# Expert weights of two mixture-of-experts blocks in loads of two megabytes instead of one

## The chip, the cores and the metric

The kernel runs on one core of a Trainium2 chip, and the figure is the device time of one execution in microseconds, the median of several runs. All arithmetic of the experts is in 32-bit floats.

## The reference, cut to what matters

Two transformer blocks run one after the other on 256 tokens of width 1024. Each ends in a layer of experts, and every expert's weights are read once from HBM:

```python
# first block: 16 experts, each takes its 32 best tokens
xg = jax.vmap(lambda hb, ib: hb[ib])(h, idx)                     # (1, 16, 32, 1024)
hid = jax.nn.silu(jnp.einsum('becd,edf->becf', xg, w_gate)) * jnp.einsum('becd,edf->becf', xg, w_up)
y = jnp.einsum('becf,efd->becd', hid, w_down) * gate[..., None]  # w_gate, w_up: 1024x2048; w_down: 2048x1024
...
# second block: 32 experts of width 512, two for each token, at most 64 rows of an expert in the fast path
hid = jax.nn.silu(xb @ w1[e]) * (xb @ w3[e])                     # w1, w3: 1024x512; w2: 512x1024
return hid @ w2[e]
```

That is 24 MB of weights for each of the 16 experts of the first block (384 MB) and 6 MB for each of the 32 of the second (192 MB); "MB" is 1,048,576 bytes here and in the prediction, where a load is spoken of. All else (attention mixers, projections, norms) needs some 115 MB.

## The kernel before

The program is four functions in a row: `block1` (mixers of the first block), `experts1`, `block2` (mixers of the second), `experts2`.

**Loads.** All weights come through `K.load` (line 211): it takes the next of a list of pools, `self.rings`, each one buffer of 8 KB in every partition, and lets SyncE's queue issue one DMA of 128 partitions by 8 KB, 1 MB. SyncE issues in order. A load waits until the readers of the buffer's last tile are done; it also waits for the load eight before it to land, since eight semaphores go round. `program` (line 2009) opens four buffers for good. `extra_ring` adds more while memory is free, `turn` rotates the list. When `experts1` begins, the list holds 19 buffers: 10 of the 11 opened ahead of the output projection of `block1`, the four, the eleventh, and four opened at that block's end. For `experts2` it holds 18: seven opened inside `block2`, seven at its end, and the four. The scheduler lets loads go ahead of their use as soon as buffers allow, so each ring is filled while the output projection and the router ahead of its experts still run.

**First block's experts** (`experts1`, line 1248 on): groups `gq` of four experts. `rows` gathers the tokens of a group into `xg` (two copies, `bufs=2`) by one-hot matmuls `gx`. For each expert, `G` (gate) and `U` (up) take eight loads each; each load feeds four matmuls that fill four stripes of 32 partitions (each is shown as two instructions in the trace). `hs` = silu(G)·U, `hT` its transpose, and `Yp` takes eight loads of `w_down`. These come from HBM as two rows of 4 KB for each partition, since `w_down` lies there as in the reference; `w_gate` and `w_up` have rows of 8 KB. The last expert takes `w_down` by halves of the columns, in four rows of 2 KB. Then `cmb` matmuls add the result to `x1`.

**Second block's experts** (`experts2`, line 1760 on): eight turns `e0` of four experts, each in two steps `c` of two experts; a step takes four loads of `w1` into `G`, four of `w3` into `U`, four of `w2` into `Yp`, all in rows of 8 KB that `layout` has packed.

Of the kernel before, what the change touches and what calls it, by code (L numbers as in the profile page):

```python
# [9 lines left out]
F32 = mybir.dt.float32  # L10
# [90 lines left out]
def layout(I):  # L101
# [37 lines left out]
    w = I["w_in"][0]  # L139
# [13 lines left out]
    A["w_choose"] = wpack(np.concatenate([I["w_group_2"][0], I["w_expert_2"][0]], 1), (0,), 36)[0]  # L153
    for n in ("w_gate", "w_up", "w_down"):
        A[n] = I[n][0]
    w = I["w_in_2"][0]
# [10 lines left out]
    for n in ("w1", "w3"):  # L167
        A[n] = I["moe_" + n + "_2"][0].reshape(16, 2, 4, 2, 128, 512).transpose(0, 2, 4, 3, 1, 5).reshape(64, 128, 2048)
    A["w2"] = I["moe_w2_2"][0].reshape(16, 2, 2, 2, 128, 2, 512).transpose(0, 5, 2, 4, 3, 1, 6).reshape(64, 128, 2048)
    return {k: np.ascontiguousarray(v) for k, v in A.items()}  # L170
# [3 lines left out]
class K:  # L174
# [14 lines left out]
    def setup(self):  # L189
        nc = self.nc  # L190
        self.rings = [self.pool("ring") for _ in range(self.ring_n)]
        self.nload = 0
# [68 lines left out]
    def extra_ring(self, n, head=0):  # L261

        st, old = ExitStack(), self.rings
        k = len(old) - head
        self.rings, self.nload = old[:k] + [self.pool("ring2", st=st) for _ in range(n)] + old[k:], 0
        st.callback(lambda: setattr(self, "rings", old))
        return st

    def turn(self, n):

        self.rings, self.nload = self.rings[n:] + self.rings[:n], 0

# [210 lines left out]
def block1(S):  # L483
# [667 lines left out]
    main.close()  # L1151
    ring = S.extra_ring(11)

# [5 lines left out]
    st.close()  # L1159
    S.turn(S.ring_n)  # L1160
    S.turn(1)
    ring.callback(S.extra_ring(4).close)
    return x1, ring


def experts1(S, x1, ring):
# [81 lines left out]
    for gq in range(4):  # L1248
        xg = lb.tile([128, 8, 128], F32, name="xg", bufs=2)

# [12 lines left out]
        for ee in range(4):  # L1263
# [4 lines left out]
            for wn, p in (("w_gate", G), ("w_up", U)):  # L1268
                for k in range(8):
                    wt = S.load(I[wn][e, 128 * k:128 * k + 128, :], wn)  # L1270
                    for j in range(4):
                        mm(p[32 * j:32 * j + 32, :], xg[:, k, s_], wt[:, 512 * j:512 * j + 512], k == 0, k == 7)
            if ee == 0:
# [28 lines left out]
            if not last:  # L1302
                for i in range(8):
                    wt = S.load(I["w_down"][e, 256 * i:256 * i + 256, :].rearrange("(k p) d -> p k d", k=2), "w_down")
                    for kk in range(2):
                        j, b = (2 * i + kk) // 4, (2 * i + kk) % 4
                        for n in range(2):
                            lo = 64 * kk + 32 * n
                            mm(Yp[lo:lo + 32, :], hT[:, b, 32 * j:32 * j + 32], wt[:, 1024 * kk + 512 * n:1024 * kk + 512 * n + 512], i == 0, i == 7)
# [52 lines left out]
def block2(S, x):  # L1362
# [301 lines left out]
    ring.close()  # L1664
    ring = S.extra_ring(7)

# [27 lines left out]
    st.close()  # L1694
    S.turn(S.ring_n)
    more = S.extra_ring(7, S.ring_n)
    ring.callback(more.close)
# [19 lines left out]
def experts2(S, x, ring, out):  # L1717
# [127 lines left out]
    def gate_up(xg, e0, c):  # L1845
# [3 lines left out]
        for wn, p in (("w1", G), ("w3", U)):  # L1849
            for k in range(0, 8, 2):  # L1850
                wt = S.load(I[wn][2 * (e0 + 2 * c) + k // 2], wn)
                for kk in range(2):
                    for e in range(2):
# [14 lines left out]

    def down(Y, hT, e, n, qs=(0, 2)):

        for q in qs:
            wt = S.load(I["w2"][2 * e + 2 * n + q // 2], "w2")
            for b in range(2):
                for i in range(2):
                    lo = 1024 * b + 512 * i
                    pe(Y[64 * i:64 * i + 64, n, :], hT[:, q + b, 64 * i:64 * i + 64], wt[:, lo:lo + 512], q + b == 0, q + b == 3)

# [26 lines left out]
    for e0 in range(0, 32, 4):  # L1904
# [34 lines left out]
        Y = py.tile([128, 2, 512], F32, name="Yp")  # L1939
        down(Y, hT, 30, 0)  # L1940
        yb = [evac(Y, 0, gs[:, 1:2])]
        down(Y, hT, 30, 1, (0,))
        for k in range(4):
            add(k, [(ya, sel[:, 0]), (yb, sel[:, 1])])
        down(Y, hT, 30, 1, (2,))
        yb.append(evac(Y, 1, gs[:, 1:2]))
# [18 lines left out]
    with tc.If(nover > 0):  # L1965
# [7 lines left out]
        with tc.For_i(0, 16, 1) as i:  # L1973
            def weights(wn, ab, name):

                t = so.tile([128, 2, 2, 512], F32, name=name, tag=name)
                nc.sync.dma_start(t, I[wn].rearrange("(i c) p f -> i c p f", c=4)[bass.ds(i, 1), ab].rearrange("a p f -> p (a f)"))
                return t
# [64 lines left out]
```

## Time and profile before

| | |
|---|---|
| median of 3 runs | 2084.6 us (2080.07 to 2085.31) |
| profiled execution, its own time | 2084.64 us |
| its span (first to last instruction) | 2082.8 us |
| TensorE (PE) busy | 1704.7 us, 82% |
| HBM read | 720.96 MB (10^6 bytes), 347 GB/s over the span |
| chain that ended last | DMA 48%, PE 37%, VectorE 8%, ScalarE 3% |
| loads of the experts | w 192, w_gate 128, w_up 128, w_down 128, 1024 KB each |

The span falls into stretches: `block1` up to about 389 us, `experts1` to about 1308, `block2` to about 1616, `experts2` to the end. The median and the profiled execution agree to 0.04 us, so sums are made against 2084.64 us, which is the span and 1.84 us around it.

### The profile page before, as it was taken

The page shows a single profiled execution, that of the slowest core. Times are in us where ns is not written, and L with a number is a line of the kernel's source. Part 1 is how long each engine was busy: PE and PEld are TensorE (multiplying, and loading weights), DVE is VectorE, ACT ScalarE, POOL GpSimd, SP SyncE. Part 2 cuts the span into 40 slices and gives each one's busy share as a digit, 9 for nine tenths or more (in the row PEclk, how much of TensorE's full clock was granted, in tenths as well). Part 3 has the DMA queues.
Part 4 walks back from the last instruction along what each step waited for, and adds up shares of the span by engine and source line. Part 5 has one row for each costly group of instructions (what it writes and reads, how often), then busy time and mean ns, then how long its engine had stood idle before and what let it go on. Part 6 is the DMA issues. An engine that isn't in the chain of part 4 may idle for free.

```text
span 2082.8 us, 25800 instructions
## 1 busy us (share of the span) xinstructions
PE 1704.7 (82%) x10570; PEld 845.0 (41%) x10570; DVE 672.3 (32%) x1327; ACT 448.6 (22%) x797; POOL 211.9 (10%) x273
## 2 busy tenths in 40 slices
PE   5979999876776667666676776899998999999997
PEld 1657557411211112111121111788998444444443
DVE  4797674311111111001011110699655112222212
ACT  4632325200010001000010000476644111111111
POOL 2334432000000000000000000243101000000000
PEclk8989999887787787877877778899999999999998
DMA  7356649799999999999999999434557799999995
GB/s 308 114 192 263 219 169 393 320 424 423 425 425 425 425 423 425 424 424 425 425 425 425 424 424 418 174 134 144 218 200 310 323 426 427 426 426 427 426 427 224
DMA packets 120842, 723.75 MB, mean 347 GB/s; under 512 B 11456, under 2 KB 13248, under 8 KB 50448
## 3 DMA queue, kind: packets, MB, share of 16 engines
q1 hardware_dynamic: 119600, 717.97, 84.2%
q0 software_dynamic: 1120, 4.08, 0.6%
q8 instruction: 85, 1.39, 0.2%
q14 instruction: 37, 0.30, 0.0%
HBM read 720.96 MB, written 1.05 MB: 347 GB/s over the span
## 4 chain that ended last, share of the span: by engine, by line
DMA 48%; PE 37%; DVE 8%; ACT 3%; issue 2%; POOL 1%; SPq 0%; DVEq 0%; ACTq 0%; POOLq 0%
DMA w_up<-in_w_up_dram 14%; DMA w_gate<-in_w_gate_dram 13%; DMA w_down<-in_w_down_dram 13%; DMA w<-in_w_dram 8%; PE pj L253 7%; PE Yp L1809 4%; PE U L1809 3%; PE G L1809 3%; PE pw L253 2%; PE U L1179 2%; DVE tmp L781 1%; PE mp L514 1%; PE ya L253 1%; PE gx L1809 1%; PE yb L253 1%
## 5 line engine op out<-in xcount | busy, mean ns | idle before, releaser
L1179 PE MATMUL U<-w_up,xg 128*32 128x512 f32 x1024 | 199.8, 872 | 99.9 <-DMA w_up<-in_w_up_dram 99.9
L1179 PE MATMUL Yp<-w_down,hT 128*32 128x512 f32 x1024 | 175.2, 785 | 91.5 <-DMA w_down<-in_w_down_dram 81.3
L1179 PE MATMUL G<-w_gate,xg 128*32 128x512 f32 x1024 | 159.0, 664 | 55.1 <-DMA w_gate<-in_w_gate_dram 54.9
L1285 DVE TENSOR_TENSOR hs<-hs,U 128x512 f32<-128x512 f32 x16 | 11.0, 687 | 469.6 <-PE U L1179 469.6
L1179 PEld LDWEIGHTS U<-w_up,xg 128*32 128x32 f32 x1024 | 24.7, 127 | 274.2 <-DMA w_up<-in_w_up_dram 243.1
L253 PE MATMUL pj<-uh,whi 128*128 128x256 f32 x408 | 118.1, 290 | 3.2 <-ACT uh L1409 3.2
L1809 PE MATMUL U<-w,xg 128*64 128x512 f32 x512 | 115.3, 595 | 5.8 <-DMA w<-in_w_dram 5.8
L253 PE MATMUL pj<-uh,wlo 128*128 128x256 f32 x408 | 116.8, 286 | 1.1 <-DVE wlo L235 1.1
L253 PE MATMUL pj<-ul,whi 128*128 128x256 f32 x408 | 115.7, 284 | 0.0
L1809 PE MATMUL Yp<-w,hT 128*64 128x512 f32 x512 | 113.8, 596 | 2.2 <-DVE ysl L1882 1.6
L1179 PEld LDWEIGHTS Yp<-w_down,hT 128*32 128x32 f32 x1024 | 25.5, 124 | 215.5 <-DMA w_down<-in_w_down_dram 187.4
L1809 PE MATMUL G<-w,xg 128*64 128x512 f32 x512 | 112.6, 592 | 0.0
L1299 ACT COPY ys<-Yp 128x256 f32<-128x256 f32 x17 | 6.3, 372 | 486.7 <-DVE ys L1298 486.7
L234 ACT CAST whi<-win 128x1024 fp32r<-128x1024 f32 x72 | 75.0, 1045 | 95.4 <-PE pj L253 61.6
L1179 PE MATMUL cmb<-seln,ys 128*128 128x256 f32 x256 | 85.6, 470 | 11.6 <-DVE ys L1298 9.5
L1422 POOL DMA_DIRECT2D dist<-in_dist_dram x1 | 0.6, 608 | 908.8 <-PE tq L436 908.8
L1179 PEld LDWEIGHTS G<-w_gate,xg 128*32 128x32 f32 x1024 | 27.8, 114 | 152.7 <-DMA w_gate<-in_w_gate_dram 108.6
L1298 DVE COPY ys<-Yp 128x256 f32<-128x256 f32 x17 | 7.2, 424 | 246.3 <-PE Yp L1179 246.3
L1295 DVE SCALAR_TENSOR_TENSOR x<-cmb,modT,x 128x256 f32<-128x256 f32 x128 | 59.4, 484 | 68.1 <-PE cmb L1179 68.1
L1179 PEld LDWEIGHTS cmb<-seln,ys 128*128 128x128 f32 x256 | 50.2, 221 | 76.2 <-DVE ys L1298 29.7
L253 PEld LDWEIGHTS pj<-uh,whi 128*128 128x128 f32 x408 | 77.6, 191 | 5.2 <-ACT uh L1409 3.5
L253 PEld LDWEIGHTS pj<-uh,wlo 128*128 128x128 f32 x408 | 77.5, 190 | 2.5 <-DVE wlo L235 1.5
(564 smaller groups left out, 2942.3 us busy)
## 6 DMA issues: line engine op xcount, KB each, us to landing
w<-in_w_dram SPq DMA_DIRECT2D x192, 1024.0 KB, 19.5
w_gate<-in_w_gate_dram SPq DMA_DIRECT2D x128, 1024.0 KB, 19.6
w_up<-in_w_up_dram SPq DMA_DIRECT2D x128, 1024.0 KB, 19.6
w_down<-in_w_down_dram SPq DMA_DIRECT2D x128, 1024.0 KB, 19.6
wmod<-in_w_mod_dram SPq DMA_DIRECT2D x48, 1024.0 KB, 6.0
win<-in_w_in_dram SPq DMA_DIRECT2D x36, 1024.0 KB, 4.9
wout<-in_w_out_dram SPq DMA_DIRECT2D x8, 1024.0 KB, 6.4
wrnn<-in_w_rnn_out_dram SPq DMA_DIRECT2D x8, 640.0 KB, 7.2
```

Of the source, the lines that this page charges most:

```text
L234: self.nc.scalar.copy(hi, x)
L253: self.nc.tensor.matmul(out, a(k), b(k), start=(n == 0), stop=(n == 3 * K - 1))
L514: nc.tensor.matmul(out, l, r, start=a, stop=b)
L781: nc.vector.tensor_tensor(tv, X[:, 0:i, 0:i], bc(Lt[:, None, 0:i, i], [128, i, i]), op=ALU.mult)
L1179: nc.tensor.matmul(out, l, r, start=a, stop=b)
L1285: nc.vector.tensor_tensor(hs, hs, U, op=ALU.mult)
L1295: nc.vector.scalar_tensor_tensor(x1[:, k, :], pc, S.modT[:, 40 + k, 0:1], x1[:, k, :], op0=ALU.mult, op1=ALU.add)
L1298: nc.vector.tensor_copy(ys[:, 0:256], Y[:, 0:256])
L1299: nc.scalar.copy(ys[:, 256:512], Y[:, 256:512])
L1422: nc.gpsimd.dma_start(dist, I["dist"])
L1809: tc.keep_in_program_order(nc.tensor.matmul(o, l, r, start=a, stop=b))
```

## The change

- Weights of all experts are packed by `layout` so that 16 KB stand in a row for each partition; a load is 128 rows of 16 KB, 2 MB. `w_gate` and `w_up` take four loads for an expert instead of eight, `w_down` four whole rows instead of eight pairs of 4 KB rows. The last expert of the first block keeps eight loads of 1 MB for `w_down`, now one row of 8 KB each instead of four of 2 KB. In the second block `w1`, `w3` and `w2` take two loads for a step instead of four; the last step keeps four loads of 1 MB for `w2`.
- The list of buffers becomes a list of windows of 16 KB, each a pool used as a small ring (`windows`); `room` puts a load of 2 MB, or two of 1 MB, into a window. All other loads stay at 1 MB.
- The counts: 10 + 4 + 6 buffers of 8 KB for the first block's experts, that is 10 windows (20 MB instead of 19), and 6 + 8 + 4, 9 windows, for the second's (18 MB as before). `xg` of the first block has one copy instead of two.

```diff
+    for n in ("w_gate", "w_up"):
+        A[n] = I[n][0].reshape(16, 4, 2, 128, 2048).transpose(0, 1, 3, 2, 4).reshape(64, 128, 4096)
+    w = I["w_down"][0].reshape(16, 4, 4, 128, 1024).transpose(0, 1, 3, 2, 4).reshape(64, 128, 4096)
+    w[60:] = I["w_down"][0, 15].reshape(2, 8, 128, 2, 512).transpose(3, 0, 2, 1, 4).reshape(4, 128, 4096)
...
+    def windows(self, n, st):
+        out = []
+        for i in range(0, n, 2):
+            m = min(2, n - i)
+            out.append((self.pool("ring", st=st).ring(8192 * m), m))
+        return out
+
+    def room(self, need, name):
+        i, used = self.place
+        while used + need > self.rings[i][1]:
+            i, used = (i + 1) % len(self.rings), 0
+        self.place = (i, used + need)
+        return self.rings[i][0].tile([128, 2048 * need], F32, name=name)
+
     def load(self, src, name):
-        pool = self.rings[self.nload % len(self.rings)]
-        self.nload += 1
-        t = pool.tile([128, 2048], F32, name=name, tag="w")
+        t = self.room(2 if math.prod(src.shape[1:]) > 2048 else 1, name)
...
-    ring = S.extra_ring(11)
+    ring = S.extra_ring(10)
...
-    ring.callback(S.extra_ring(4).close)
+    ring.callback(S.extra_ring(6).close)
...
-        xg = lb.tile([128, 8, 128], F32, name="xg", bufs=2)
+        xg = lb.tile([128, 8, 128], F32, name="xg", bufs=1)
...
-                    wt = S.load(I[wn][e, 128 * k:128 * k + 128, :], wn)
+                    if k % 2 == 0:
+                        wt = S.load(I[wn][4 * e + k // 2], wn)
...
-                for i in range(8):
-                    wt = S.load(I["w_down"][e, 256 * i:256 * i + 256, :].rearrange("(k p) d -> p k d", k=2), "w_down")
+                for i in range(4):
+                    wt = S.load(I["w_down"][4 * e + i], "w_down")
...
-                    wt = S.load(I["w_down"][e, 512 * i:512 * i + 512, 512 * n:512 * n + 512].rearrange("(k p) d -> p k d", k=4), "w_down")
+                    wt = S.load(I["w_down"][4 * e + 2 * n + i // 2, :, 2048 * (i % 2):2048 * (i % 2) + 2048], "w_down")
...
-    ring = S.extra_ring(7)
+    ring = S.extra_ring(6)
...
-    more = S.extra_ring(7, S.ring_n)
+    more = S.extra_ring(8, S.ring_n // 2)
...
-            for k in range(0, 8, 2):
-                wt = S.load(I[wn][2 * (e0 + 2 * c) + k // 2], wn)
+            for k in range(0, 8, 4):
+                wt = S.load(I[wn][e0 + 2 * c + k // 4], wn)
...
+    def down(Y, hT, e, n, q=0, c=4):
+        wt = S.load(I["w2"][e + n, :, 1024 * q:1024 * (q + c)], "w2")
```

The order of SyncE's queue where the first block's ring is filled, before: from the eleventh load of the ring on. The first four rows below go into the four lasting buffers, which wait (DVE, Pool) until the output projection has split its weights; the fifth into the eleventh extra buffer, the next four into the buffers opened last, and the last row is the first buffer used again.

```order
L216 DMA w_up<-in_w_up_dram 128x2048 [waits DMAHW5_49,DVE_49,Pool_49]
L216 DMA w_up<-in_w_up_dram 128x2048 [waits DMAHW6_49,DVE_49]
L216 DMA w_up<-in_w_up_dram 128x2048 [waits DMAHW7_49,DVE_49,Pool_49]
L216 DMA w_up<-in_w_up_dram 128x2048 [waits DMAHW0_49,DVE_49]
L216 DMA w_up<-in_w_up_dram 128x2048 [waits DMAHW1_49]
L216 DMA w_up<-in_w_up_dram 128x2048 [waits DMAHW2_49,PE_49]
L219 DMA w_down<-in_w_down_dram 128x2x1024 [waits DMAHW3_49]
L219 DMA w_down<-in_w_down_dram 128x2x1024 [waits DMAHW4_49,PE_49]
L219 DMA w_down<-in_w_down_dram 128x2x1024 [waits DMAHW5_49]
L219 DMA w_down<-in_w_down_dram 128x2x1024 [waits DMAHW6_49,PE_49]
```

The same queue and place with the change: the fourth window of the ring, then the two lasting ones, the fifth extra one, the three opened last, and the first window used again.

```order
L235 DMA w_gate<-in_w_gate_dram 128x4096 [waits PE_49]
L235 DMA w_up<-in_w_up_dram 128x4096 [waits DMAHW1_49,DMAHW7_49,DMAHW0_49,DVE_49]
L235 DMA w_up<-in_w_up_dram 128x4096 [waits DMAHW2_49,DVE_49]
L235 DMA w_up<-in_w_up_dram 128x4096
L235 DMA w_up<-in_w_up_dram 128x4096 [waits PE_49]
L235 DMA w_down<-in_w_down_dram 128x4096 [waits DMAHW3_49,PE_49]
L235 DMA w_down<-in_w_down_dram 128x4096 [waits DMAHW4_49]
L235 DMA w_down<-in_w_down_dram 128x4096 [waits DMAHW5_49,PE_49]
```

What moved: ten loads stand for nineteen, and the lasting buffers are met after 8 MB instead of 10.

PE's queue at the last step of the second block's experts, before: the four loads of `w3` and what follows on them.

```order
L1809 MATMUL U<-w_12623,xg 64x512 [waits DMAHW7_49]
L1809 MATMUL U<-w_12623,xg 64x512 x3
L1809 MATMUL U<-w_12629,xg 64x512 [waits DMAHW0_49]
L1809 MATMUL U<-w_12629,xg 64x512 x3
L1809 MATMUL U<-w_12635,xg 64x512 [waits DMAHW1_49]
L1809 MATMUL U<-w_12635,xg 64x512 x3
L1809 MATMUL U<-w_12641,xg 64x512 [waits DMAHW2_49]
L1809 MATMUL U<-w_12641,xg 64x512 x3
L1809 MATMUL cmb<-sel,ysh 128x256 [waits Activation_49]
```

The same place of PE's queue with the change:

```order
L1829 MATMUL U<-w_12026,xg 64x512 [waits DMAHW7_49]
L1829 MATMUL U<-w_12026,xg 64x512 x7
L1829 MATMUL U<-w_12036,xg 64x512 [waits DMAHW0_49]
L1829 MATMUL U<-w_12036,xg 64x512 x7
L1829 MATMUL cmb<-sel,ysh 128x256 [waits Activation_49]
```

What moved: eight matmuls hang on the last landing instead of four, as in every other `G`, `U` and `Yp`. On VectorE and GpSimd the order of instructions is the same; on ScalarE three copies of one gather moved by a few places.

PE's queue at the gather for the next group in the first block's experts (after the fourth expert's `U`), before:

```order
L1288 MATMUL hT<-cst,hs 128x128 x3
L382 MATMUL gx<-oh,x1t 128x128 [waits PE_49]
L382 MATMUL gx<-oh,x1t 128x128 x3
L1179 MATMUL Yp<-w_down,hT 32x512 [waits DMAHW3_49,DVE_49]
L1179 MATMUL Yp<-w_down,hT 32x512 x3
L382 MATMUL gx<-oh,x1t 128x128 x4
```

And with the change:

```order
L1309 MATMUL hT<-cst,hs 128x128 x3
L401 MATMUL gx<-oh,x1t 128x128 [waits PE_49]
L401 MATMUL gx<-oh,x1t 128x128 x7
L401 MATMUL gx<-oh,x1t 128x128 [waits DVE_49]
L401 MATMUL gx<-oh,x1t 128x128 x5
L1198 MATMUL Yp<-w_down,hT 32x512 [waits DMAHW7_49]
```

What moved: more of the gather stands ahead of the first `w_down`; in both it stands behind the group's last `U`, which is the last reader of the old `xg`.

## Rows read from the trace of the kernel before

**Rows 1.** Page: the span in 40 equal slices (tenths; then GB/s)
```profile
DMA  7356649799999999999999999434557799999995
GB/s 308 114 192 263 219 169 393 320 424 423 425 425 425 425 423 425 424 424 425 425 425 425 424 424 418 174 134 144 218 200 310 323 426 427 426 426 427 426 427 224
```

**Rows 2.** Windows: busy us (instructions) of each engine, PE clock, DMA share, GB/s
```profile
442.00:1280.00 838.00, 582.51 (x3090) 132.87 (x3086) 82.17 (x166) 41.71 (x96) 0.00 (x0) 0.77 1.02 424
...
1622.00:1890.00 268.00, 260.10 (x1355) 115.00 (x1355) 52.71 (x103) 40.08 (x66) 0.00 (x0) 1.00 1.00 419
1890.00:2048.00 158.00, 148.73 (x760) 62.81 (x758) 30.50 (x59) 22.17 (x35) 0.00 (x0) 1.00 1.01 427
```

**Rows 3.** Chain that ended last, by time: start us, us, what
```profile
466.44 19.58 DMA w_gate<-in_w_gate_dram
486.08 19.54 DMA w_up<-in_w_up_dram
508.17 17.76 DMA w_down<-in_w_down_dram
...
1301.38 1.98 PE Yp L1179 x8
...
2047.90 1.96 PE U L1809 x8
```

**Rows 4.** Waits of SyncE's queue, 442 to 1280: us in total, times, longest
```profile
SPq L216 <- DMA w_gate<-in_w_gate_dram: 232.6, 112, 2.9
...
SPq L216 <- DMA w_down<-in_w_down_dram: 124.1, 70, 2.9
SPq L219 <- PE U L1179: 90.9, 33, 6.8
```

**Rows 5.** DMA view of 466:503, 505.5:523, 1280:1290 and 1700:2040
```profile
DMA packets 2169, 15.80 MB, mean 427 GB/s; under 512 B 241, under 2 KB 241, under 8 KB 241
...
DMA packets 1896, 7.31 MB, mean 418 GB/s; under 512 B 112, under 2 KB 112, under 8 KB 1896
...
DMA packets 2055, 4.08 MB, mean 408 GB/s; under 512 B 61, under 2 KB 61, under 8 KB 2055
...
DMA packets 19898, 144.99 MB, mean 426 GB/s; under 512 B 2213, under 2 KB 2213, under 8 KB 2213
```

**Rows 6.** DMA queues in 1288:1298: packets, MB, share of 16 engines
```profile
q8 instruction: 1, 0.02, 0.6%
```

**Rows 7.** First block's ring: DMA idle (windows), then issues of SyncE (timeline)
```profile
380.00:390.00 10.00, 9.34 (x44) 8.22 (x48) 4.50 (x19) 1.69 (x5) 4.55 (x12) 0.50 0.05 19
...
326.65 7.89 SPq L216 DMA_DIRECT2D w_gate<-in_w_gate_dram  x8
...
350.07 0.33 SPq L216 DMA_DIRECT2D w_up<-in_w_up_dram  x1
...
363.33 0.80 SPq L216 DMA_DIRECT2D w_up<-in_w_up_dram  x2
...
390.66 0.37 SPq L219 DMA_DIRECT2D w_down<-in_w_down_dram  x1
...
392.36 0.37 SPq L219 DMA_DIRECT2D w_down<-in_w_down_dram  x1
```

**Rows 8.** Second block's ring: the same two views
```profile
1610.00:1620.00 10.00, 5.32 (x24) 5.24 (x25) 5.92 (x32) 0.83 (x3) 0.00 (x0) 0.58 0.20 84
...
1624.65 0.33 SPq L216 DMA_DIRECT2D w<-in_w_dram  x1
...
1626.37 0.33 SPq L216 DMA_DIRECT2D w<-in_w_dram  x1
```

**Rows 9.** Timeline of ScalarE and PE: a gather, and the next group's first matmuls
```profile
572.41 0.46 ACT L388 ACTIVATE xg<-gx,modT,A 128x128 f32<-128x128 f32 x1 [25.12 <-PE gx L382]
...
576.45 0.45 ACT L388 ACTIVATE xg<-gx,modT,A 128x128 f32<-128x128 f32 x1
...
591.29 1.04 PE L1179 MATMUL G<-w_gate,xg 128*32 128x512 f32 x2
```

More of the change, by code (lines that the diff above doesn't have):

```diff
@@ L153, in layout @@
     A["w_choose"] = wpack(np.concatenate([I["w_group_2"][0], I["w_expert_2"][0]], 1), (0,), 36)[0]
-    for n in ("w_gate", "w_up", "w_down"):
-        A[n] = I[n][0]
+    for n in ("w_gate", "w_up"):
+        A[n] = I[n][0].reshape(16, 4, 2, 128, 2048).transpose(0, 1, 3, 2, 4).reshape(64, 128, 4096)
+    w = I["w_down"][0].reshape(16, 4, 4, 128, 1024).transpose(0, 1, 3, 2, 4).reshape(64, 128, 4096)
+    w[60:] = I["w_down"][0, 15].reshape(2, 8, 128, 2, 512).transpose(3, 0, 2, 1, 4).reshape(4, 128, 4096)
+    A["w_down"] = w
     w = I["w_in_2"][0]
@@ L167, in layout @@
     for n in ("w1", "w3"):
[L168 to L169 removed]
+        A[n] = I["moe_" + n + "_2"][0].reshape(16, 2, 2, 4, 128, 512).transpose(0, 2, 4, 3, 1, 5).reshape(32, 128, 4096)
+    A["w2"] = I["moe_w2_2"][0].reshape(16, 2, 4, 128, 2, 512).transpose(0, 4, 3, 2, 1, 5).reshape(32, 128, 4096)
     return {k: np.ascontiguousarray(v) for k, v in A.items()}
@@ L190, in setup @@
         nc = self.nc
-        self.rings = [self.pool("ring") for _ in range(self.ring_n)]
-        self.nload = 0
+        self.rings = self.windows(self.ring_n, self.st)
+        self.place = (0, 0)
         self.keep = self.pool("keep")
@@ L264, in extra_ring @@
         k = len(old) - head
-        self.rings, self.nload = old[:k] + [self.pool("ring2", st=st) for _ in range(n)] + old[k:], 0
+        self.rings, self.place = old[:k] + self.windows(n, st) + old[k:], (0, 0)
         st.callback(lambda: setattr(self, "rings", old))
@@ L269, in turn @@
     def turn(self, n):
-        self.rings, self.nload = self.rings[n:] + self.rings[:n], 0
+        self.rings, self.place = self.rings[n:] + self.rings[:n], (0, 0)
     def router(self, ps, w, A, B, bias, name):
@@ L1159, in block1 @@
     st.close()
-    S.turn(S.ring_n)
+    S.turn(S.ring_n // 2)
     S.turn(1)
-    ring.callback(S.extra_ring(4).close)
+    ring.callback(S.extra_ring(6).close)
     return x1, ring
@@ L1302, in experts1 @@
             if not last:
-                for i in range(8):
-                    wt = S.load(I["w_down"][e, 256 * i:256 * i + 256, :].rearrange("(k p) d -> p k d", k=2), "w_down")
-                    for kk in range(2):
-                        j, b = (2 * i + kk) // 4, (2 * i + kk) % 4
+                for i in range(4):
+                    wt = S.load(I["w_down"][4 * e + i], "w_down")
+                    for b in range(4):
                         for n in range(2):
-                            lo = 64 * kk + 32 * n
-                            mm(Yp[lo:lo + 32, :], hT[:, b, 32 * j:32 * j + 32], wt[:, 1024 * kk + 512 * n:1024 * kk + 512 * n + 512], i == 0, i == 7)
+                            lo = 64 * (b % 2) + 32 * n
+                            mm(Yp[lo:lo + 32, :], hT[:, b, 32 * i:32 * i + 32], wt[:, 1024 * b + 512 * n:1024 * b + 512 * n + 512], i == 0 and b < 2, i == 3 and b > 1)
                 ys = lb.tile([128, 512], F32, name="ys", tag="h2", bufs=4)
@@ L1694, in block2 @@
     st.close()
-    S.turn(S.ring_n)
-    more = S.extra_ring(7, S.ring_n)
+    S.turn(S.ring_n // 2)
+    more = S.extra_ring(8, S.ring_n // 2)
     ring.callback(more.close)
@@ L1849, in gate_up @@
         for wn, p in (("w1", G), ("w3", U)):
-            for k in range(0, 8, 2):
-                wt = S.load(I[wn][2 * (e0 + 2 * c) + k // 2], wn)
-                for kk in range(2):
+            for k in range(0, 8, 4):
+                wt = S.load(I[wn][e0 + 2 * c + k // 4], wn)
+                for kk in range(4):
                     for e in range(2):
@@ L1867, in across @@
         return hT
[L1869 to L1876, printed above, removed]
+    def down(Y, hT, e, n, q=0, c=4):
+        wt = S.load(I["w2"][e + n, :, 1024 * q:1024 * (q + c)], "w2")
+        for b in range(c):
+            for i in range(2):
+                lo = 1024 * b + 512 * i
+                pe(Y[64 * i:64 * i + 64, n, :], hT[:, q + b, 64 * i:64 * i + 64], wt[:, lo:lo + 512], q + b == 0, q + b == 3)
     def evac(Y, n, g):
@@ L1939, in experts2 @@
         Y = py.tile([128, 2, 512], F32, name="Yp")
-        down(Y, hT, 30, 0)
+        for q in (0, 2):
+            down(Y, hT, 30, 0, q, 2)
         yb = [evac(Y, 0, gs[:, 1:2])]
-        down(Y, hT, 30, 1, (0,))
+        down(Y, hT, 30, 1, 0, 2)
         for k in range(4):
             add(k, [(ya, sel[:, 0]), (yb, sel[:, 1])])
-        down(Y, hT, 30, 1, (2,))
+        down(Y, hT, 30, 1, 2, 2)
         yb.append(evac(Y, 1, gs[:, 1:2]))
```

5 lines of the change are left out of this document (3 added, 2 removed).

## The prediction

> **What bounds the kernel now.** I read the page's slices first. From slice 9 to slice 25, and again from slice 33 to slice 39, the DMA engines are busy nine tenths or more and move 418 to 427 GB/s [rows 1]. In the first of these stretches, the first block's experts, PE is busy only 583 of 838 us; the second lies inside 1622 to 2048 us [rows 2]. The chain of waits agrees: in the first block it is handed from landing to landing (eight w_gate in 19.58 us, eight w_up in 19.54) and PE adds only its last eight matmuls, at 1301 and at 2048 us [rows 3]. In the second block PE is busy 260 of 268 us up to 1890 us, since it first eats the ring's stock; yet DMA streams at its full rate behind it from about 1627 us on, and the chain ends on its last w3 load [rows 2, 3]. So both blocks end when a fixed number of megabytes has come through a saturated stream, and what counts is the pace of the stream, the moment it becomes continuous, and what follows its last landing.
>
> The pace depends on the row size. In stretches where all weights come in 8 KB rows the trace shows 427 GB/s, with 4 KB rows (w_down) 418, with 2 KB rows (the last expert's w_down, at 1280 us) 408; over 340 us of the second block, all in 8 KB rows, 426 [rows 5]. For a load of 1 MB, 1,048,576 bytes, that is 2.456, 2.509, 2.570 and 2.461 us. Each row is one packet, so an engine carries 8, 16 or 32 for such a load: from 8 to 16 costs 53 ns, 6.6 ns a packet; from 16 to 32 costs 61 ns, 3.8 ns a packet.
>
> **The change part by part.** *Rows of 16 KB.* No row of the weights' queue has this size, so the cost is bounded. An engine would carry 4 packets for 1 MB instead of 8. At 6.6 ns each that saves 26 ns, at 3.8 ns it saves 15; were the whole cost of eight packets to go, 53; and the other end is nothing gained, or a loss (rivals). I take 26, the step between the two nearest sizes: 2.430 us for 1 MB, or 431 GB/s.
>
> Here a page bears on it. The rows already show 427 GB/s over 37 us and 426 over 340 [rows 5]. The Trainium skill, HBM Reference, section Specifications (TRN2), says that a core streaming alone reaches about 425 GB/s and is held there by its 16 DMA engines; by that, nothing is left above the pace of 8 KB rows. The trace is already slightly past that figure, and whether it can go on is what the first rival asks.
>
> The terms, first block. The ring holds 19 loads when DMA falls idle: 19 GB/s from 380 to 390 us [rows 7]. From the first reuse on 365 of the 384 remain: 240 of gate and up, 117 of w_down in 4 KB rows (8 x 15, less the 3 in the ring), 8 of the last expert's w_down.
> - gate and up: 240 x 0.026 = 6.2 us less.
> - w_down, 4 KB to 16 KB: 117 x (2.509 - 2.430) = 9.2 us less.
> - last expert's w_down, 2 KB to 8 KB, still 1 MB a load: 8 x (2.570 - 2.456) = 0.9 us less.
> - the ring: SyncE issues the first reuse at 390.66 us, when PE has used one load, and the next at 392.36 [rows 7]. A window is free only after both, 1.7 us later; but 20 MB lie in the ring instead of 19, worth 2.43 us. Together 0.7 us less. This asks that 20 MB are in by about 392 us. Now the two lasting windows come after 8 MB, not 10. Those 8 MB, issued from 326.65 us behind w_out's last loads, take 8 x 2.43 = 19 us and land by about 350; the first lasting window, free when its second buffer is at 350.07, lands by 357; the second is free only when the last w_out buffer is, at 363.33 [rows 7]. DMA idles some 6 to 8 us there; the last five windows, 10 x 2.43 = 24 us, run from 365 to about 389. It fits by 3 us. If it did not, each us missed costs one.
>
> After the stream's last landing nothing changes in this block, since its last loads stay at 1 MB: eight matmuls, 1.98 us [rows 3]. The up phase of the last expert ends about 2 us later, under the 20 us in which its w_down lands.
>
> Second block. 18 loads lie in the ring, DMA falls to 84 GB/s in 1610 to 1620, and the first reuse is issued at 1624.65, the second at 1626.37 [rows 8]. The chain ends on the last w3 load, 170 loads later (192 less 18 and less the four of w2).
> - 170 x 0.026 = 4.4 us less.
> - first window free after two loads: 1.7 us more.
> - behind the last w3 landing stand 16 matmuls instead of 8: 1.96 us more [rows 3], in the open. w2's four loads need 9.8 us from there and are still under the chain of hs, hT and cmb.
> Together 0.7 us less.
>
> The rest costs nothing. One copy of xg: the gather's last write is at 576.45 us and the next group's first gate matmul at 591.29 [rows 9], and PE's queue has the gather behind the last reader of the old copy before and after; without that cover it would cost that gather, about 5 us, three times. SyncE's queue waits today for the landing of the load eight before (233 us on w_gate and 124 on w_down, against 91 on U) [rows 4]; with eight loads of 2 MB allowed in flight and 20 MB of ring its waits will be for PE, but 16 MB in flight are more than the 8 of now. Half the semaphore packets fall away, which I leave uncounted. block1 and block2 keep their 1 MB loads.
>
> Sum: 6.2 + 9.2 + 0.9 + 0.7 + 0.7 = 17.7 us. From the profiled execution's own 2084.64 us, which is the median too, that gives **2066.9 us**. With 15 ns the same sum is 12 us (2072.5), with 53 ns it is 32 us (2053).
>
> **The rivals.**
> *The stream is at its ceiling* with 8 KB rows: 16 KB rows are cut into two packets, or come no faster. For it: 426 to 427 GB/s is the most that any long stretch shows, and no larger row stands in this queue [rows 5]. Against it: 2, 4 and 8 KB each gained 2 to 2.5%, with no sign of levelling. Then gate, up and the second block gain nothing, w_down gains 117 x 0.053 = 6.2 us, the last expert 0.9, the ring 0.7, the second block loses 3.7: 4.1 us less, 2080.5 us. It is the page's figure, named above, worked out as a mechanism of this kernel.
>
> *A 16 KB packet is dearer than two of 8 KB*: this one ends slower. The only 16 KB packets in the trace belong to the instruction queue; one of them took 0.6% of 16 engines in 10 us, 0.96 us [rows 6], where two 8 KB packets take about 0.61 (an eighth of 2.456 us each). It goes elsewhere than into weight tiles, so I hold it for weak evidence. It decides from 2.464 us for 1 MB, 426 GB/s: there the 527 loads of 2 MB halves (240 + 117 + 170) give back all of w_down's gain. At the pace of today's 4 KB rows, 418 GB/s, it is 527 x 0.045 = 24 us slower, 2108 us; at 0.96 us a packet it would be some 2800.
>
> *The ring starves*: windows come free in steps of 2 MB, and DMA idles once per expert for the 1.7 us that a window comes later [rows 7]: 15 x 1.7 = 26 us against the 17.7, 2093 us. Against it: PE is busy 583 of 838 us [rows 2] and holds two or three windows of ten.
>
> *PE becomes the bound in the second block*: PE was busy 260 of 268 us there [rows 2], so DMA's gain may not be taken up; then only the first block gains, 17.0 us, and the tails cost 3.7: 2071 us.
>
> **How the numbers follow.** Forecast as summed: 0.66. PE as the bound: 0.07. Ceiling: 0.15. Dearer packets: 0.08. Starving ring: 0.04. Faster by over 0.3%, about what a measurement here can tell from no change, means below 2078.4 us: the forecast, the PE case and a small part of the ceiling case, 0.76. Within 0.3%: most of the ceiling case and a little of the others, 0.13. Slower: 0.11. The range runs from the 53 ns end, not quite reached since some cost of a packet must stay, to just past the ceiling case: 2055 to 2083 us; some 0.14 lies above it and little below.
>
> **What would show it.** GB/s of 431 or so in the slices where it is 424 to 427; the 59 us of an expert of the first block (24 loads) shrinking by about 1 us; one packet for each 16 KB row in the count (8 KB packets instead would be the ceiling case); SyncE waiting for PE instead of for landings; DMA idle near 360 us and not after 394; 16 matmuls of U behind the last w3 landing. Wrong would be: a DMA share under 1 inside the two stretches (starving), or a pace of 426 GB/s or less with the share at 1 (dearer packets).

## The result and the profile after

The changed kernel takes 2068.4 us (median of 4 runs, 2065.9 to 2070.4) where the kernel before takes 2082.4 beside it: ratio 0.9928, 95% interval 0.9916 to 0.9940, so 12 to 17 us faster. A second comparison, of five runs, gave 2067.1 us and 0.9924 (0.9911 to 0.9938). The forecast was 2066.9 us, in a range of 2055 to 2083. The profiled execution took 2070.4 us itself, its span is 2068.6 us.

Page of the changed kernel: the DMA engines in 40 slices, tenths and GB/s, and all their packets. It answers to [rows 1].

```profile
DMA  7256648899999999999999999434548899999994
GB/s 310 103 204 260 209 183 345 356 431 430 431 431 431 431 431 430 430 431 432 430 430 431 430 431 426 156 121 156 199 172 350 341 432 431 429 430 431 430 430 203
DMA packets 61798, 723.69 MB, mean 350 GB/s; under 512 B 6945, under 2 KB 8737, under 8 KB 11121
```

The slices that stood at 423 to 427 GB/s stand at 429 to 432, in both blocks. The count of packets fell from 120,842 to 61,798 for the same megabytes.

Windows of the changed kernel over the two stretches of [rows 2] (busy us and count of PE, PEld, DVE, ACT, POOL, then PE clock, DMA share, GB/s), and the DMA view of the first stretch (queue, packets, MB, share of 16 engines).

```profile
442.00:1268.00 826.00, 540.37 (x3094) 143.02 (x3090) 82.33 (x166) 41.72 (x96) 1.14 (x2) 0.82 1.01 431
1622.00:1890.00 268.00, 260.02 (x1352) 114.61 (x1350) 53.05 (x103) 39.39 (x65) 0.00 (x0) 1.00 1.01 430
1890.00:2034.00 144.00, 134.14 (x698) 59.02 (x696) 28.95 (x57) 20.20 (x32) 0.00 (x0) 1.00 1.01 430
```

```profile
DMA packets 24539, 355.61 MB, mean 431 GB/s; under 512 B 2721, under 2 KB 2721, under 8 KB 2721
q1 hardware_dynamic: 24509, 355.17, 100.5%
q8 instruction: 24, 0.39, 0.2%
```

The DMA share is 1.01 all along, as before, and more bytes come through. Of the 24,509 packets of the weights' queue 2721 are the small ones under 512 bytes; the other 21,788 carry 355.17 MB, some 16,300 bytes each: a 16 KB row (16,384 bytes) is one packet. One of them takes 826 us x 16 x 1.005 / 21,788 = 610 ns.

The chain that ended last (start us, us, what); each landing now stands for eight loads of 2 MB. It answers to [rows 3].

```profile
446.32 39.03 DMA w_gate<-in_w_gate_dram
485.43 38.78 DMA w_down<-in_w_down_dram
524.27 38.80 DMA w_up<-in_w_up_dram
563.13 38.86 DMA w_gate<-in_w_gate_dram
602.06 40.12 DMA w_down<-in_w_down_dram
...
875.80 40.15 DMA w_up<-in_w_up_dram
...
1149.49 40.14 DMA w_gate<-in_w_gate_dram
...
2031.31 3.68 PE U L1829 x16
```

From 446.32 to 602.06 us four steps bring 64 loads' worth of 1 MB: 155.74 / 64 = 2.433 us each. The step at 602.06 is 1.3 us longer than its neighbours; so are those at 875.80 and 1149.49, about 273 us apart. Behind the last w3 landing stand 16 matmuls, 3.68 us.

To see where the time went, each profiled execution is cut at five marks that are the same work in every kernel: the first G of the first block's experts, the end of their last Yp, the first matmul `pj` of the second block, the first G of its experts, the end of their last U, and the end of the span.

| us | to first G | G to last Yp | to first pj | to second G | G to last U | to the end | span |
|---|---|---|---|---|---|---|---|
| before | 388.7 | 914.7 | 14.7 | 304.7 | 427.2 | 32.9 | 2082.8 |
| changed | 390.1 | 899.4 | 12.1 | 307.0 | 426.3 | 33.7 | 2068.6 |

The first block's experts gave 15.3 us, the second's 0.8. The rest, work whose code the change leaves alone, is 1.4 and 2.3 and 0.7 longer and 2.6 shorter; what the experiments say of it stands under *The rest at nothing* below.

### The profile page after: what moved, and what is told of

Same layout as the page of the kernel before. It is cut to its first block, busy times and chain, and to the rows that moved or that the text cites. A ratio compares the mean times of both kernels' runs of the same rounds, so it can differ in the third digit from the quotient of the medians.

```text
span 2068.6 us, 25205 instructions
## 1 busy us (share of the span) xinstructions
PE 1662.2 (80%) x10570; PEld 856.2 (41%) x10570; DVE 672.2 (32%) x1327; ACT 448.9 (22%) x797; POOL 211.6 (10%) x273
## 2 busy tenths in 40 slices
DMA packets 61798, 723.69 MB, mean 350 GB/s; under 512 B 6945, under 2 KB 8737, under 8 KB 11121
## 4 chain that ended last, share of the span: by engine, by line
DMA 47%; PE 39%; DVE 8%; ACT 3%; issue 2%; POOL 1%; SPq 0%; DVEq 0%; ACTq 0%; POOLq 0%
DMA w_up<-in_w_up_dram 15%; DMA w_down<-in_w_down_dram 14%; DMA w_gate<-in_w_gate_dram 13%; PE pj L272 7%; PE Yp L1829 5%; PE U L1829 4%; PE G L1829 4%; DMA w<-in_w_dram 4%; PE pw L272 2%; PE gx L1829 2%; DVE tmp L800 1%; PE mp L533 1%; PE ya L272 1%; PE yb L272 1%; PE cmb L1829 1%
## 5 line engine op out<-in xcount | busy, mean ns | idle before, releaser
L1198 PE MATMUL U<-w_up,xg 128*32 128x512 f32 x1024 | 174.1, 814 | 126.9 <-DMA w_up<-in_w_up_dram 126.9
L1198 PE MATMUL Yp<-w_down,hT 128*32 128x512 f32 x1024 | 160.3, 757 | 88.1 <-DMA w_down<-in_w_down_dram 79.4
L1198 PE MATMUL G<-w_gate,xg 128*32 128x512 f32 x1024 | 165.3, 698 | 57.6 <-DMA w_gate<-in_w_gate_dram 57.6
L1198 PEld LDWEIGHTS U<-w_up,xg 128*32 128x32 f32 x1024 | 33.4, 129 | 262.9 <-DMA w_up<-in_w_up_dram 166.5
L1198 PEld LDWEIGHTS Yp<-w_down,hT 128*32 128x32 f32 x1024 | 31.1, 125 | 198.7 <-DMA w_down<-in_w_down_dram 130.7
L1198 PE MATMUL cmb<-seln,ys 128*128 128x256 f32 x256 | 79.9, 428 | 12.8 <-DVE ys L1319 9.4
L272 PEld LDWEIGHTS pj<-ul,whi 128*128 128x128 f32 x408 | 78.6, 193 | 0.5 <-issue 0.3
## 6 DMA issues: line engine op xcount, KB each, us to landing
w_gate<-in_w_gate_dram SPq DMA_DIRECT2D x64, 2048.0 KB, 38.9
w_up<-in_w_up_dram SPq DMA_DIRECT2D x64, 2048.0 KB, 38.9
```

Of the source, the lines that this page charges most:

```text
L272: self.nc.tensor.matmul(out, a(k), b(k), start=(n == 0), stop=(n == 3 * K - 1))
L1198: nc.tensor.matmul(out, l, r, start=a, stop=b)
```

## Experiments

Theories. **A, the row:** the stream's pace goes by the size of the row, that is by the number of packets, and nothing else. **B, the load:** fewer and larger loads, with 16 MB in flight instead of 8 and half the semaphores, are what gained. Beside them the terms of the prediction's sum stand to be tried one by one: ring, first reuse, tail, and the bound in the second block.

**The changed kernel again** (unaltered, on the same chip as the 8 KB rows, w_down alone and the halved last load; the ring of 18 MB, the 8 KB rows in the second block and the five halved loads ran on another chip and are set against it by their ratios to the kernel before).

> The changed kernel again, unaltered, as the reference for the runs beside it on the same chip. Measured so far 2068.4 us (2065.9 to 2070.4) against 2082.4 of the kernel before, ratio 0.993. Expected: the same, 2066 to 2071 us, and the three short stalls of the weight stream about 273 us apart again (steps of the chain of about 40.1 us instead of 38.8).

Measured: 2067.1 us, as expected; the three stalls are there again.

**Rows of 8 KB in the same loads.** Two rows per partition for each load:

```diff
+def halves(w):
+    return w.reshape(-1, 128, 2, 2048).transpose(0, 2, 1, 3)
...
-                        wt = S.load(I[wn][4 * e + k // 2], wn)
+                        wt = S.load(I[wn][4 * e + k // 2].rearrange("a p f -> p a f"), wn)
```

(the same for w_down, w1, w3 and w2).

> The changed kernel, with each 2 MB load brought in two 8 KB rows per partition instead of one 16 KB row, in both blocks' experts; as many loads, windows and waits as in the changed kernel. Theory A, the size of the packet: 240 + 117 + 170 loads' worth of 1 MB lose 0.026 us each, 13.7 us, so 2081 to 2083 us, and the slices show 426 to 427 GB/s. Theory B, fewer and larger loads (fewer semaphores, 16 MB in flight instead of 8) are what gained: no change against the changed kernel, 2068 us and 430 GB/s.

Measured: 2078.5 us (10 runs), ratio to before 0.9975 (0.9966 to 0.9985), 11.4 us slower than the changed kernel. DMA view of the first stretch:

```profile
DMA packets 45746, 352.91 MB, mean 427 GB/s; under 512 B 2691, under 2 KB 2691, under 8 KB 2691
```

427 GB/s with the same loads, windows and semaphores: theory A holds, B falls. The bytes in flight are not quite the same: a load lands 32.5 us after its issue instead of 38.9, which at these rates is some 13.9 MB (10^6 bytes) in flight instead of 16.8. In the kernel before it was 8.4, and there 8 KB rows move 427 GB/s as well, so the bytes in flight do not set the pace. It is also what the prediction gave for a stream that gains nothing from 16 KB rows (2080.5 us, 4.1 us less than before; measured 4.4 less). Of A's 13.7 us 11.4 came: the saving for a row of 16 KB is a little smaller than the 26 ns taken.

**w_down alone, in the kernel before.** 1 MB loads as before, rows of 8 KB instead of 4 KB (2 KB in the last expert):

```diff
-                    wt = S.load(I["w_down"][e, 256 * i:256 * i + 256, :].rearrange("(k p) d -> p k d", k=2), "w_down")
+                    wt = S.load(I["w_down"][8 * e + i], "w_down")
```

> The kernel before, with w_down alone repacked so that its 1 MB loads come in 8 KB rows (4 KB before, 2 KB in the last expert). Number of loads, ring and the second block as before. Theory A, the size of the packet: 117 x 0.053 + 8 x 0.114 = 7.1 us less, 2075.3 us, with no slice at 418 GB/s in the first block's experts and 427 throughout. Theory B, the number and size of the loads: no change, 2082.4 us.

Measured: 2076.0 us (6 runs), ratio 0.9967 (0.9955 to 0.9979), 6.9 us less than before (4 to 9 by the interval). A again: the term of w_down, 7.1 us, is there with no load made larger. Chain of this kernel:

```profile
446.19 19.56 DMA w_down<-in_w_down_dram
465.81 19.56 DMA w_gate<-in_w_gate_dram
485.43 19.56 DMA w_up<-in_w_up_dram
...
622.80 20.67 DMA w_down<-in_w_down_dram
```

w_down's step is now as long as the others. Nine steps of 8 MB from 446.19 to 622.80 give 176.61 / 72 = 2.453 us for 1 MB in 8 KB rows, against 2.433 in 16 KB rows: 20 ns.

**The stream alone.** No computation; seven stages of 64 MB in rows and loads of different sizes:

```diff
+    stage("rows8k", 1, 1)
+    stage("rows16k", 2, 1)
+    stage("rows32k", 4, 1)
+    stage("pair8k", 2, 2)
+    stage("quad4k", 2, 4)
+    stage("oct2k", 2, 8)
+    stage("again16k", 2, 1)
```

(MB of a load, rows per partition).

> The stream by itself: every part of the computation is left out, and only loads run, 64 MB each in seven stages one after the other: 8 KB rows in 1 MB loads, 16 KB rows in 2 MB loads, 32 KB rows in 4 MB loads, then 2 MB loads of two 8 KB, four 4 KB, eight 2 KB rows per partition, and 16 KB rows again. Theory A, the pace goes by the size of the row alone: 427, 431, 433, 427, 418, 408, 431 GB/s, packets of 309, 611, 1215, 309, 159, 84, 611 ns. Theory B, by the size of the load: 2 MB loads all at 431 or so, 1 MB at 427. Rival for 32 KB: cut into two packets of 16 KB, then 431. Of the short stalls 273 us apart: between two of them the queue of instructions brings eight packets of 16 KB (24 in 826 us). If these cause the stalls, there are none here, where hardly any instruction runs; if the memory causes them, three or four in some 1070 us.

Windows inside the seven stages, in their order (after the length: busy us of DVE and POOL, PE clock, DMA share, GB/s), and the DMA view of the third:

```profile
20.00:150.00 130.00, 0.00 (x0) 0.00 (x0) 1.00 1.01 422
160.00:300.00 140.00, 0.00 (x0) 0.00 (x0) 1.00 1.01 429
320.00:450.00 130.00, 0.00 (x0) 0.00 (x0) 1.00 1.00 432
480.00:600.00 120.00, 0.00 (x0) 0.00 (x0) 1.00 1.01 422
630.00:760.00 130.00, 0.00 (x0) 0.00 (x0) 1.00 1.02 410
790.00:940.00 150.00, 0.00 (x0) 0.00 (x0) 1.00 1.05 388
980.00:1100.00 120.00, 0.00 (x0) 0.00 (x0) 1.00 1.01 429
```

```profile
q1 hardware_dynamic: 1920, 56.10, 100.3%
```

The first and the fourth stage decide: 8 KB rows give 422 GB/s in loads of 1 MB and of 2 MB alike. Theory A once more, and the gain goes on to 32 KB rows (432), which are one packet each: 1920 packets, 208 of them small, for 56.1 MB. All rates lie 0.2 to 5% under those forecast from the kernel, most at 2 KB; why the bare stream is slower is open. The mean packet in its records takes 89, 164, 314, 615 and 1217 ns from 2 to 32 KB: 602 ns for the last 16 KB. At that slope alone an engine carries 16,384 / 602 = 27.2 bytes per ns, sixteen 435 GB/s, and 13 ns a packet come on top. The chain does not show the stalls here, but the landings do not have them: in some 1070 us two came 0.7 to 0.8 us late and none 1.2, where a clock of 273 us would have brought three or four.

One thing more is to be read here. How long SyncE stays in one issue (ns, least, median, most; then when), in the second and the fourth stage, and then in the 8 KB kernel's first stretch:

```profile
L31 SPq DMA_DIRECT2D rows16k<-in_w_gate_dram x32: 327/328/328, 144.9 to 280.5; - x32
L31 SPq DMA_DIRECT2D pair8k<-in_w_gate_dram x32: 367/4616/16336, 436.2 to 600.5; - x32
...
L243 SPq DMA_DIRECT2D w_gate<-in_w_gate_dram x56: 406/4504/10713, 438.7 to 1222.4; - x56
```

A load of one row per partition is issued in 0.33 us. A load of two holds SyncE for some 4.6 us, close to the 4.97 in which 2 MB come through there, although PE does nothing in this kernel. So with two rows per partition the issue itself holds back the next load. What limits it is open; the DMA share stays at 1.01, so the engines are kept busy all the same.

**Ring of 18 MB in the first block**, with the second copy of xg back:

```diff
-    ring.callback(S.extra_ring(6).close)
+    ring.callback(S.extra_ring(4).close)
...
-        xg = lb.tile([128, 8, 128], F32, name="xg", bufs=1)
+        xg = lb.tile([128, 8, 128], F32, name="xg", bufs=2)
```

> The changed kernel with one window of two buffers fewer in the first block's experts (18 MB of ring instead of 20) and the second copy of xg back. The prediction's ring term says that each MB in the ring when the stream becomes continuous is worth one MB of stream, 2.43 us: 2 x 2.43 = 4.9 us slower than the changed kernel, about 2072 us, all of it between the first G of the first block and its last w_down. Rival: the ring's size is worth nothing, because the refill ends only when the first reuse begins: no change, 2067 us. The second copy of xg is expected to give nothing back in either case.

Measured: 2074.3 us, ratio 0.9954 (0.9938 to 0.9970) against 0.9924 of the changed kernel, 6 us slower, give or take 4; from G to the last Yp 905.4 us instead of 899.4 to 900.6. The ring's term holds, 2.4 to 3 us for 1 MB. Two things changed at once here, so the second copy of xg is not measured alone; but 4.9 us were forecast for the ring by itself, and nothing was given back against that. The windows before the first reuse, of the smaller ring and then of the changed kernel:

```profile
380.00:390.00 10.00, 9.49 (x47) 7.95 (x51) 4.41 (x18) 2.32 (x5) 4.55 (x12) 0.50 0.36 152
```

```profile
380.00:390.00 10.00, 7.89 (x36) 7.79 (x36) 5.27 (x20) 0.47 (x2) 4.55 (x12) 0.50 1.01 430
```

The smaller ring is full at about 384 us and DMA idles; the larger one is still filling.

**8 KB rows in the second block alone** (the edit of the first experiment, for w1, w3 and w2 only).

> The changed kernel, the second block's 2 MB loads alone in two 8 KB rows per partition again. Stream-bound second block (the forecast): 170 x 0.022 (the step measured in the first block; 0.026 by the prediction) = 3.7 to 4.4 us slower than the changed kernel, 2071 us, and G to U of the second block 430 us instead of 426.3. The rival that PE is the bound there: no change, 2067 us.

Measured: 2072.0 us, ratio 0.9942 (0.9925 to 0.9959), 3.7 us slower by the ratios, which the total alone can't tell from nothing. The piece can: G to last U 429.2 us instead of 426.3, and PE's waits for loads there add up to 8.4 us instead of 6.3. The second block ended by its stream as forecast, so the gain was taken up.

**The last w3 load in two halves:**

```diff
+                cut = e0 == 28 and c == 1 and wn == "w3" and k == 4
...
+                    if cut and kk % 2 == 0:
+                        wt = S.load(I[wn][e0 + 2 * c + k // 4, :, 1024 * kk:1024 * kk + 2048], wn)
```

> The changed kernel, with the very last w3 load of 2 MB cut into two of 1 MB (8 KB rows), so that only 8 matmuls of U instead of 16 stand behind the last landing. The prediction's tail term: 16 matmuls took 3.68 us behind the landing, 8 took 1.96, so about 1.7 us less than the changed kernel, 2066.7 us. The rival, that PE is what sets the end there or that w2 lands late: no change, 2068.4 us.

Measured: 2066.4 us, ratio 0.9920 (0.9906 to 0.9933). The total can't tell 0.7 us from nothing or from 1.7. The piece can: G to last U took 424.7 us instead of 426.2 to 426.3, 1.6 us less. Its chain:

```profile
1999.10 3.65 PE U L1829 x16
...
2009.52 7.02 PE Yp L1829 x32
2016.54 6.87 PE G L1829 x32
2023.41 7.11 PE U L1829 x32
```

After the landing at 1999.10 PE never waits for a load again: all 32 matmuls of the last U run in one piece. The tail's term was right. PE is not yet the bound of the block, though: up to that landing it still waits for loads. PE's waits for loads in the second block (us in total, times, longest), of the changed kernel and then of this one:

```profile
PE U L1829 <- DMA w<-in_w_dram: 6.3, 6, 1.6
...
PE U L1829 <- DMA w<-in_w_dram: 5.0, 5, 1.7
```

Without them either kernel would take some 420 us from G to the last U. So a faster stream could at most give back 6.3 us there in the changed kernel, and 5.0 with the last load halved.

**Five loads halved**, the last w3 and, in both blocks, the first load and the one that reuses its window, so that the first reuse waits for one load used and not two:

```diff
+                    cut = e == 0 and wn == "w_gate" and k < 2
+                    if cut:
+                        wt = S.load(I[wn][0, :, 2048 * k:2048 * k + 2048], wn)
...
+                cut = (e0, c, wn, k) in ((0, 0, "w1", 0), (0, 1, "w3", 4), (28, 1, "w3", 4))
```

> The changed kernel with five loads of 2 MB cut into two of 1 MB each: the first of each block's experts and the one that comes back into the same buffers (so that the first reuse waits for one load used instead of two), and the very last w3. By the prediction's terms: 1.7 us for the first reuse in each block, 1.7 us for the tail, less 0.2 for 10 MB in shorter rows: 4.9 us less than the changed kernel, 2062 us. If the first reuse is worth nothing, only the tail's 1.7: 2065.4 us.

Measured: 2065.1 us, ratio 0.9909 (0.9892 to 0.9926); against the changed kernel's 0.9924 this can't be told from the tail's gain alone. G to last Yp took 900.6 us and G to last U 426.1: nothing gained, and in the second block the 1.4 us that the halved last load alone had gained (424.7) are lost again. The first reuse did come 1.7 us sooner after the first G (2.0 us instead of 3.7 in both blocks), but the stream then started thinly. The windows where it starts in the second block, of this kernel (first G at 1606.7 us) and then of the changed kernel run again (1607.1):

```profile
1612.00:1616.00 4.00, 4.00 (x22) 1.38 (x20) 0.00 (x0) 0.60 (x1) 0.00 (x0) 1.00 1.03 377
1616.00:1620.00 4.00, 4.00 (x20) 1.29 (x18) 0.00 (x0) 0.00 (x0) 0.00 (x0) 1.00 1.00 350
```

```profile
1612.00:1616.00 4.00, 4.00 (x22) 1.31 (x20) 0.00 (x0) 0.60 (x1) 0.00 (x0) 1.00 0.84 344
1616.00:1620.00 4.00, 4.00 (x20) 1.29 (x18) 0.00 (x0) 0.00 (x0) 0.00 (x0) 1.00 1.01 434
```

With the DMA share at 1 it moved 377 and 350 GB/s for 8 us, where the changed kernel was at 434 in the second of these windows. The packets themselves took longer: in their records 749 ns instead of 611 for 16 KB between 1616 and 1620. PE's waits for loads in the second block add up to 6.2 us, as in the changed kernel. So the term of the first reuse was dearer on paper than on the chip; why the packets are slow when the stream opens with small loads is open.

**Where the stalls come from.** No computation; 160 loads of 2 MB in 16 KB rows alone, then 160 more while PE runs tiny matmuls:

```diff
+    t = stage("quiet", 160)
+    nc.tensor.matmul(p[:, 0:32], t[:, 0:32], z[:, 0:32], start=True, stop=True)
+    for i in range(6000):
+        nc.tensor.matmul(p[:, 0:32], z[:, 0:32], z[:, 32:64], start=True, stop=True)
+    t = stage("fetching", 160)
```

> What the three short stalls of the changed kernel come from (steps of 40.1 us among steps of 38.8, 273 us apart; PE's instructions come in packets of 16 KB, 24 of them in 826 us, so eight between two stalls). All of the reference's computation is left out: 160 loads of 2 MB in 16 KB rows with nothing else, then 160 more while PE runs 6000 tiny matmuls of 32 columns. Theory A, the instruction packets delay single DMA engines and a landing waits for the slowest: the first half goes in even steps of about 38.9 us for 16 MB, without a stall; in the second half some 47 packets for 12000 instructions give a stall of about 1.2 us for every eight, five or six in all. Theory B, something of the memory or the queue with a clock of its own: two stalls in the first 780 us, 273 us apart, and no more than three in the second half.

Its chain (start us, us, what), and its queue of instructions over the whole span:

```profile
591.56 39.18 DMA quiet<-in_w_gate_dram
...
949.09 39.33 DMA fetching<-in_w_gate_dram
988.43 40.64 DMA fetching<-in_w_gate_dram
1029.09 40.42 DMA fetching<-in_w_gate_dram
...
1150.90 39.29 DMA fetching<-in_w_gate_dram
...
1391.86 39.15 DMA fetching<-in_w_gate_dram
```

```profile
q8 instruction: 93, 1.52, 0.4%
```

In 780 us without PE's instructions every step after the first is even (39.14 to 39.37 us), though two stalls 273 us apart would have fallen there: theory B of the stalls falls. PE had twice the instructions expected (24,000, each matmul as two with a weight load each), so 93 packets of 16 KB instead of 47 were fetched, all but one between 795 and 1370 us; 11 of the 15 steps in that time are 1.2 to 1.5 us longer, and all of them together 16.7 us. That is one stall for some eight packets, as theory A has it, and 0.18 us of stream for each packet; when PE's work ends the steps are even again. Why eight, which would be eight engines taking turns, can't be read, since the records do not name the engine.

Two sections of the Trainium skill, DMA: Bandwidth & Descriptors, describe what would do this: under Queues, rings and completion order, an engine alternates between the queues that have work for it, a packet at a time; under Why a DMA increments its semaphore by 16 and not by 1, a transfer counts as landed only when all its engines have finished. These runs fit both, though they do not show single engines: the bytes moved fall only from 428 to 425 GB/s, 0.7%, while the 15 steps from landing to landing grow by 16.7 us, 2.8%, as they would if each landing waited for the engine furthest behind.

All pieces side by side:

| us | to first G | G to last Yp | to first pj | to second G | G to last U | to the end | span |
|---|---|---|---|---|---|---|---|
| changed, again | 387.2 | 900.6 | 12.4 | 306.9 | 426.2 | 34.8 | 2068.1 |
| 8 KB rows | 389.1 | 906.5 | 12.1 | 307.0 | 429.2 | 33.3 | 2077.0 |
| w_down alone | 387.9 | 907.9 | 12.2 | 304.7 | 427.1 | 33.2 | 2072.8 |
| last w3 halved | 388.6 | 899.2 | 12.1 | 305.9 | 424.7 | 34.1 | 2064.6 |
| ring of 18 MB | 388.0 | 905.4 | 12.4 | 306.9 | 426.4 | 34.4 | 2073.5 |
| 8 KB, second block | 389.5 | 899.3 | 12.1 | 304.6 | 429.2 | 34.2 | 2068.8 |
| five halved | 386.2 | 900.6 | 12.4 | 307.6 | 426.1 | 34.4 | 2067.3 |

## Why the prediction was right

**The bound.** Right. With the same loads, 8 KB rows alone cost 11.4 us; the time is set by the stream in both blocks.

**The pace of 16 KB rows: right mechanism, size a little off.** Taken were 26 ns for 1 MB, 2.430 us. Measured in undisturbed steps: 2.453 against 2.433 us, 20 ns. Over the whole first stretch the 8 KB kernel's 906.5 us against 899.4 make 7.1 us for 357 loads' worth, 20 ns again (16 by the second run's 900.6), where the sum had 9.3. In the second block it is 429.2 against 426.3, 2.9 us for 170, where the sum had 4.4. That is the mis-sized term: some 3.7 us of the 17.7. The trace of before read 427 GB/s for 8 KB rows, a rounded figure, which is 2.456; half of the shortfall is in that rounding.

**w_down:** 9.2 + 0.9 us for its way to 16 KB (8 KB in the last expert); the part from 4 to 8 KB, 7.1 us by the same rates, measured 6.9 by medians, and 6.8 from G to last Yp.

**The ring and the first reuse.** Forecast 2.43 less and 1.7 more, 0.7 net. The 8 KB kernel, which has the ring of 20 MB but no faster rows than the kernel with w_down alone, is 1.4 us shorter from G to last Yp. A MB of ring is worth 2.4 to 3 us; the later first reuse cost less than 1.7, and taking it back gained nothing. The ring filled in time, with the 3 us to spare that were forecast: DMA idled near 360 us (185 GB/s from 355 to 365), was at 430 GB/s until 390 and done by 391, and the first reuse came at 393.8.

**The second block:** forecast 0.7 us less, measured 0.8, of these terms: 2.9 less for the rows (4.4 forecast), 1.6 more for the tail (1.96), and some 0.5 more, what is left over, for the first window (1.7). Two terms were too large on opposite sides, so that 0.7 came out as 0.8 is partly luck.

**The rest at nothing.** One copy of xg cost nothing that shows: in the first stretch SyncE waits for landings and hardly for PE (the lines below), and the DMA share is 1.01. The pieces outside the experts differ by up to 3 us, and two of them go with the granted clock.

- To the first pj. At the end of the first block's experts PE waited 2.79 us for the last w_down and did its last eight Yp matmuls in 1.98 us at 1.2 GHz before [rows 3]; after, it waited 0.73 us and did them in 1.1 at 2.4 GHz. The piece behind them took 14.7 us before, and 12.1 to 12.4 in all eight kernels whose w_down was packed anew. So the 2.6 us may belong to the change, where the prediction had nothing; there is only one trace of the kernel before to set against them.
- From the first pj to the second G. The kernel before and the one with w_down alone took 304.7 us, the one with 8 KB rows in the second block 304.6, the six others with the new loads 305.9 to 307.6. In the second 50 us of this piece the granted clock was 1.00 in the first three and 0.97 in the six. Since one kernel with the new loads is among the three, the change does not fix it; why the clock fell there is open.

**The sum.** 17.7 us forecast, 14.0 and 15.8 measured in the two comparisons. The time itself came nearer (2066.9 against 2068.4) than the gain, since the sum started from 2084.64 us, 2.2 above the median of four runs: that is luck.

**The rivals.** The ceiling falls: 431 GB/s over 826 us. The Trainium skill's figure, HBM Reference, section Specifications (TRN2), about 425 GB/s for a core alone, is what this kernel reached before, not what holds it: these runs show 431 in the kernel, and 432 with 32 KB rows. A nearer limit is that of the Trainium skill, DMA: Bandwidth & Descriptors, section Specifications, 435 GB/s for the fabric; the packets' slope of 602 ns for 16 KB gives the same, and no stretch of 100 us or more here passed it. The dearer packet falls: 610 ns for 16 KB. The 0.96 us of the instruction queue's packet [rows 6] said nothing on the weights. The starving ring falls: the share is 1.01. PE as the bound of the second block was the nearest, but PE still waited 6.3 us for loads there, and slower rows made the block longer.

**The signatures.** All were seen but one. SyncE's waits in the first stretch:

```profile
SPq L235 <- DMA w_up<-in_w_up_dram: 255.9, 57, 5.8
SPq L235 <- DMA w_down<-in_w_down_dram: 251.6, 56, 5.8
SPq L235 <- DMA w_gate<-in_w_gate_dram: 251.5, 56, 5.8
SPq L235 <- PE G L1198: 2.7, 9, 0.4
```

They were to turn from landings to PE; they did the opposite. The step that failed: that 20 MB of ring less what PE holds is under the 16 MB that eight loads may have in flight. A load lands in 38.9 us, eight times the 4.87 of one load, so eight of the ten windows are in flight; PE holds less than the two others, since it eats a load as soon as it lands, and the load eight before lands last. It changed nothing in the time, for the stream is full either way.

The 91 us for PE's U in the kernel before [rows 4] were misread as well. They stand on w_down, in that stretch the only load with two rows per partition, whose issue held SyncE for up to 8.4 us (median 1.5); with w_down alone in one row per partition its issue took 0.33 us and these waits were gone, though PE's work was the same. The view of SyncE's waits names what last signalled while the issue lasted, which need not be what ended it. With 8 KB rows in the same loads it names PE again, 110.7 us for cmb, which reads no weights, and 103.8 for G, and again the issue itself lasts, 4.5 us for each load. With SyncE held there, some 6.6 loads are under way instead of eight, and a load lands 32.5 us after its issue instead of 38.9.

## What to carry to other kernels

When a stream of weights sets the end, take its pace from stretches that differ only in the length of the contiguous row, and lengthen the row first: in the kernel 4 to 8 KB gave 2.2% and 8 to 16 KB 0.8%, and from 16 to 32 KB the bare stream still gained 0.7%, while larger loads of the same row gave nothing. Then count what is loaded when the stream becomes continuous (2.4 to 3 us for each MB) and the matmuls that hang on the last landing. Before taking the next percent, look how far the engine behind the stream is from being the bound: add up its waits for loads, here 6.3 us in one of two blocks. And before a wait of a DMA queue is put down to an engine, look how long the issue itself took.

## What was unexpected of the hardware

- A packet's time is close to a fixed part and a slope: in the stream alone 89, 164, 314, 615, 1217 ns for 2, 4, 8, 16, 32 KB, so 13 ns and 37.6 ns a KB at the upper end.
- A load of two 8 KB rows per partition held SyncE in its issue for 4.6 us (median), one of a 16 KB row for 0.33, with no other engine at work.
- PE's instructions cost the stream time: one packet of 16 KB for about 258 instructions (24,000 in 93), and 0.18 us for each where loads of 2 MB follow one another.
- A stream that started from rest with 1 MB loads moved slowly for some us with the DMA share at 1: 350 to 377 GB/s over 8 us in the second block of the kernel with five halved loads.
- The same weights stream at 431 GB/s beside the kernel's work and at 429 alone, 8 KB rows at 427 and 422. The runs do not say why.
